# A two-layer diffusion trunk on one core: an earlier weight chunk and a one-run modulation in the first stage, and one ScalarE square moved behind branch A

## The chip, the core and the metric

The kernel runs on one core of a Trainium2 chip. The metric is device time in microseconds (us) of one execution, taken as a median of runs. Engines are named as the profile names them: PE is TensorE (matrix products), PEld its weight loads, ACT is ScalarE, DVE is VectorE, POOL is GpSimd, SP is the engine that issues nearly all DMAs.

## What is computed

Two layers over a latent stream `x` (256 tokens) and a context stream `ctx` (256 tokens), 2048 wide, all in fp32. Cut to what matters here:

```
shift, scale, gate = split(silu(c) @ w_mod[l] + b_mod[l])      # the same for the context with c_ctx
h    = rmsnorm(x, g_pre[l]) * (1 + scale) + shift              # h_c from ctx in the same way
proj = h @ w_in[l]                                             # a_u, a_v, a_g, q, k, v, b_g, c_x, c_g
y_a  = gelu(a_u) * (w_s @ rmsnorm(gelu(a_v)) + b_s) * silu(a_g)    # branch A
y_b  = window_attention(q, k, v, k_ctx, v_ctx) * silu(b_g)         # branch B
y_c  = (real part of fft2(c_x)) @ w_f * silu(c_g)                  # branch C
x    = x + gate * rmsnorm([y_a, y_b, y_c] @ w_out[l], g_post[l])   # ctx too, in the first layer only
```

## The kernel before, in words

Everything is laid out with the 2048 channels as 16 tiles of 128 (`k` = 0 to 15) and the tokens along the free axis (256 latent, 256 context). A product in fp32 is done as three passes in the PE's faster fp32r type: each operand is split into a rounded high part and a low remainder, and `mm3` (lines 428 to 430) adds high*high, low*high and high*low. Weights therefore take three steps: SP loads a 512 KB chunk into a `raw` buffer (line 383), ACT casts it to the high part `whi` (line 403), DVE subtracts to get the low part `wlo` (line 408). `Stream` hands the chunks out in a fixed order with `W.next()`; `W.emitting(512)` does cast and subtraction in halves of 512 columns, one step per `next`.

**First stage (layer 0).** The order of work on PE, ACT, DVE and SP is exactly the order in which the code is written (a manual schedule), up to `k` = 14. For each `k` the stage does four `start_av` products groups (branch A's `a_v`, one PSUM bank for each 128 tokens) and `start_au` for three heads of `a_u` (`au[0]` to `au[2]`; the third head, index 2, has its own weight chunk `ws_[2]`). Beside this, the modulation for the next tile `k + 1` is worked out: `mod_start` loads 2 MB of `w_mod` in pieces (line 162; tiles `mraw`, `macc`, `vv` for one parity of `k`, `mg`, `mgl`, `hh`, `hl` for the other), multiplies them on PE (line 169, `ps_mod`), transposes on DVE (line 173), gathers on PE (line 178, `ps_modc`), and adds biases on DVE (lines 187 to 190: `gs` and `sh`). `make_h` then makes the tile `h`: a DVE product (line 507), an ACT pass that rounds it (`hh`, line 511), a DVE pass for the remainder (`hl`, line 516). The generator is advanced by `take_in(n)`, n steps at a time; `h_next()` finishes it and makes `h`. `LOADS[k]` says how many weight chunks SP loads in step `k`, `SPLITS[k]` how many are cast and subtracted. `warm` (line 474) issues dummy bf16 products that write a bank which is overwritten later.

Before the change, the third head's first chunk is loaded and split in step `k` = 2; its products for `k` = 0, 1 and 2 stand together at the end of that step, and step 1 ends in four dummy products. The modulation that step 2 works out (for `k` = 3) is multiplied in two runs of two pieces, one after each half of the `a_v` products.

**The border of layer 1.** In the last steps of layer 1's own first stage the context stream's residual is finished in the background (`boundary_ctx`): DVE multiplies (line 1176), POOL issues DMAs that add the old stream into `yo` (line 1168), ACT squares the result (line 1185), and DVE sums the squares. Here the queue order comes from a scheduler, with `boundary_ctx` at lowered priority. Branch A begins with Gelu on ACT (lines 755 and 757), squares with a sum along the row (line 759), a power on POOL (line 459) and a scaling on DVE (line 763); PE then mixes positions (`ps_mix`, line 768). `ps_mix` and branch C's `ps_mg` (line 783; read by ACT line 445 and DVE line 446) share two PSUM banks.

Of the kernel before, what the change touches and what calls it, by code (L numbers as in the profile page):

```python
# [10 lines left out]
AF = mybir.ActivationFunctionType  # L11
# [55 lines left out]
def trunk_kernel(ctx: ExitStack, tc: tile.TileContext, xT, xhalf, cT, wss, wsl, wmod, win, wout0, wout1, const, vec, rows,  # L67
                 wmat, bs, sink, out):
    nc = tc.nc
    V, A, G, PE, DMA = nc.vector, nc.scalar, nc.gpsimd, nc.tensor, nc.sync  # L70
# [22 lines left out]
    yo = [sb([P, T], F32, f"yo{k}") for k in range(KT)]  # L93
# [180 lines left out]
    state = {"ctx": [], "phase": "", "owed": 0.0}  # L274
# [6 lines left out]
                k1=2.5, v1=2.5, q1=1, bg1=0.3, out1=1.4)  # L281
    NEAR = [0] * 14 + [1, 2, 3]

    LOADS = [1, 1, 1, 2, 1, 1, 1, 1, 1, 0, 2, 0, 1, 1, 1, 0]
    SPLITS = [1, 1, 1, 2, 0, 1, 1, 1, 1, 1, 0, 2, 0, 1, 1, 1]
    MIDDLE, EARLY = 3, 4
    LOWC = 60
    YT = 3.0
# [54 lines left out]
    class Stream:  # L343
# [75 lines left out]
        def next(self):  # L419
            self.fetch()  # L420
            pace()
            self.pos += 1
            return self.out[self.pos - 1]

    W = Stream()
# [45 lines left out]
    def warm(ps, n):  # L471

        for _ in range(n):
            PE.matmul(ps, wz[:, 0:P], wz, start=True, stop=True)
# [102 lines left out]
    def layer(l):  # L577
# [13 lines left out]
        av = [mm_ps("av") for _ in range(nt)]  # L591
# [17 lines left out]
        def start_au(k, heads=(0, 1, 2)):  # L609
            for j in heads[:3 - l]:  # L610
                if j == 2:
                    c, auw = slice((k % 8) * P, (k % 8 + 1) * P), ws_[2]
                else:
                    c, auw = slice((k % 4) * 256 + j * P, (k % 4) * 256 + (j + 1) * P), ws_[1]
                if last:
                    mm2(au[j], part(auw, c), hh[k], k)
                else:
                    mm3(au[j], part(auw, c), (hh[k], hl[k]), k == 0, k == KT - 1)
            later.tick(PASS * 512 * nt + PASS * n * 2)

        if l == 0:
            made = {}

            def mod_in(k, n=5):
                if k < KT:
                    g = made.setdefault(k, mod_start(k, 1))
                    for _ in range(n):
                        next(g, None)

            for k in range(KT):  # L630
                def take_in(n):
                    mod_in(k + 1, n)

                def splits():
                    for _ in range(SPLITS[k]):
                        W.emit()

                def h_next():

                    if k + 1 < KT:  # L640
                        mod_in(k + 1)
                        make_h(0, k + 1, rb0, [0, 1])

                if k % 2 == 0:
                    take(k)
                if k <= EARLY:
                    take_in(1)
                if k >= EARLY:
                    mod_in(k + 2, 1)
                for _ in range(LOADS[k]):  # L650
                    W.load()
                if k == 0:
                    start_av(0, range(nt))
                    take_in(3)
                    e = W.emitting(512)
                    next(e)
                    next(e)
                    take_in(2)
                    take(0, (1,))
                    start_au(0, (0,))  # L660
                    h_next()
                    list(e)
                    start_au(0, (1,))
                    warm(au[2], 3)
                elif k < MIDDLE:
                    start_av(k, range(nt // 2))
                    take_in(2)
                    start_av(k, range(nt // 2, nt))
                    take_in(1)
                    splits()  # L670
                    take_in(2)
                    start_au(k, (0,))
                    h_next()
                    start_au(k, (1,))
                    if k == 1:
                        warm(au[2], 4)
                    else:
                        ws_[2] = W.next()
                        for i in range(k + 1):
                            start_au(i, (2,))  # L680
                else:
                    start_av(k, range(nt // 2))
                    if k <= EARLY:
                        take_in(3)
                        splits()
                        take_in(2)
                        start_av(k, range(nt // 2, nt))
                        h_next()
                    else:
                        if k == KT - 2:  # L690
                            first_stage.close()
                        if k + 2 < KT:
                            banks["mod", k + 2] = banks["modc", k + 1] = ms_ps("mod")
                        splits()
                        mod_in(k + 2, 4)
                        if k + 1 < KT:
                            mod_in(k + 1)
                            make_h(0, k + 1, rb0, [0, 1])
                        mod_in(k + 2, 1)
                        start_av(k, range(nt // 2, nt))  # L700
                    if k >= KT - 2:
                        for _ in range(2):
                            with low(LAG), tc.issue_after(W.last.ins):
                                next(mods)
                    take(k, (1, 2))
                    start_au(k)
                    if k == EARLY:
                        mod_in(k + 2, 5)
# [42 lines left out]
        def branch_a():  # L751
            vt = [w2k([P, 512]) for _ in range(nt)]
            ss = sb([P, 4], F32, "ss")
            for j in range(len(au)):
                A.activation(ytmp(j), joined(au[j]) if last else au[j], AF.Gelu_apprx_tanh)
            for t in range(nt):
                A.activation(vt[t], av[t], AF.Gelu_apprx_tanh)
            for t in range(nt):
                A.activation(av[t], vt[t], AF.Square, accum_out=ss[:, t:t + 1])
            r = rstd_cols(ss[:, 0:nt], nt, 512)  # L760
            state["norm"] = state["pow"]
            for t in range(nt):
                V.tensor_scalar(out=vt[t], in0=vt[t], scalar1=r[:, t:t + 1], scalar2=None, op0=ALU.mult)
            yield 11.0 if l == 0 else 7.0
            for h in range(4):
                ps = ms_ps("mix")
                for t in range(nt):
                    PE.matmul(ps[:, t * P:(t + 1) * P], vt[t][:, h * P:(h + 1) * P], ws[:, h], start=True, stop=True)
                m = w2k([P, nt, P])
                V.scalar_tensor_tensor(out=m, in0=ps[:, 0:n].rearrange("p (t q) -> p t q", q=P),  # L770
                                       scalar=vc(l, "gsgu")[:, h:h + 1],
                                       in1=bsb[:, h].unsqueeze(1).to_broadcast([P, nt, P]),
                                       op0=ALU.mult, op1=ALU.add)
                V.tensor_tensor(out=ytmp(h), in0=ytmp(h), in1=m.rearrange("p t q -> p (t q)"), op=ALU.mult)
                yield (4.0 if h == 1 else 2.0) if l == 0 else (7.0 if h == 1 else 2.0)
# [389 lines left out]
    def boundary_ctx(acc):  # L1165

        def add(k):
            G.dma_start(yo[k][:, CTX], xhalf[1, k // 4][:, k % 4], accum_op=ALU.add)

        r = sb([P, S], F32, "rbs", 2)  # L1170
        r0 = yield from rms_of(1, acc[:, CTX], 3.2)
        A.copy(r, r0)
        acc1 = acc[:, CTX]
        for k in range(KT + LATE):
            if k < KT:
                V.tensor_tensor(out=yo[k][:, CTX], in0=yo[k][:, CTX], in1=r, op=ALU.mult)
                if k < 8:
                    add(k)
                else:
                    with tc.issue_after(state["norm"].ins):  # L1180
                        add(k)
            i = k - LATE
            if i >= 0:
                q = w2k([P, S]) if i else acc1
                A.activation(q, yo[i][:, CTX], AF.Square)
                if i:
                    V.tensor_tensor(out=acc1, in0=acc1, in1=q, op=ALU.add)
            if k % 2:
                yield YX1 if k == 7 else YC
        yield YE  # L1190
        r0 = yield from rms_of(1, acc1, 6.0)
        r = sb([P, S], F32, "rbs", 2)
        V.tensor_copy(r, r0)
        for i, k in enumerate([12, 13, 14, 15] + list(range(12))):
            make_h(1, k, r, [1])
            state["ctx"].append(k)
            if i % 2:
                yield YH
# [145 lines left out]
```

## Time and profile before

| what | us |
|---|---|
| median of 3 runs | 1138.46 (1137.81 to 1140.13) |
| the profiled execution, as timed | 1138.35 |
| its span in the trace, first to last instruction | 1136.6 |
| PE, PEld busy | 1123.4, 931.8 |
| DVE, ACT, POOL busy | 879.8, 514.4, 32.5 |

The profiled execution lies 0.11 us from the median. Times in the text are from the start of the span. A row of the timeline gives start, duration, engine, line, operation, the tile written and read, and the shapes; in brackets stands the idle time of that engine before it and what ended it. A PE product of 512 columns is shown with a duration of about 0.39 us, but products overlap: in a run of them one starts every 0.23 us. So starts are compared here, not durations.

### The profile page before, as it was taken

How to read it: one execution, taken by the hardware profiler on the slowest of the kernel's cores; microseconds unless marked ns; L12 is line 12 of the kernel's file. 1: busy time of each engine (PE TensorE's matmuls, PEld its weight loads, DVE VectorE, ACT ScalarE, POOL GpSimd, SP SyncE). 2: the span in 40 equal slices, each digit the busy share in tenths (PEclk: the TensorE clock that was granted, in tenths of full speed). 3: DMA queues.
4: the chain of work that ended last, by engine and by line, in shares of the span. 5: the costliest groups of instructions: out<-in, count | busy, mean ns of one | idle time of the engine just before them, and what ended most of it. 6: DMA issues, size and time to landing. Idle time of an engine off the chain costs nothing.

```text
span 1136.6 us, 16851 instructions
## 1 busy us (share of the span) xinstructions
PE 1123.4 (99%) x6335; PEld 931.8 (82%) x6339; DVE 879.8 (77%) x1480; ACT 514.4 (45%) x933; POOL 32.5 (3%) x39
## 2 busy tenths in 40 slices
PE   8999999999999999999999999999999999999997
PEld 3567788888898888888888888987898988888885
DVE  1545499999987887888998994396788689868884
ACT  5322422332325667632532323365655369856550
POOL 0000000000000000000000000205000000000001
PEclk9999999999999999999999999999999999999999
DMA  9999766556655343355566655268756675555972
GB/s 354 393 379 404 252 204 195 178 186 212 212 168 184 112 139 114 118 188 186 164 205 203 218 191 166 72 197 203 221 179 206 224 268 193 174 160 195 299 256 74
DMA packets 72658, 234.28 MB, mean 206 GB/s; under 512 B 8448, under 2 KB 11392, under 8 KB 72576
## 3 DMA queue, kind: packets, MB, share of 16 engines
q1 hardware_dynamic: 70272, 231.11, 61.3%
q0 software_dynamic: 2304, 2.10, 1.2%
q8 instruction: 49, 0.80, 0.3%
q14 instruction: 33, 0.27, 0.1%
HBM read 231.08 MB, written 2.10 MB: 205 GB/s over the span
## 4 chain that ended last, share of the span: by engine, by line
PE 96%; DMA 2%; DVE 0%; SPq 0%; issue 0%; ACT 0%; POOL 0%; DVEq 0%; POOLq 0%
PE ps_t L428 14%; PE ps_t L429 14%; PE ps_t L430 14%; PE ps_t L545 10%; PE ps_t L546 5%; PE ps_y L428 3%; PE ps_y L430 3%; PE ps_y L429 3%; PE ps_mod L169 2%; PE ps_av L428 2%; PE ps_cx L430 2%; PE ps_cx L428 2%; PE ps_cx L429 2%; PE ps_av L429 2%; PE ps_av L430 2%; PE ps_tp L917 2%
## 5 line engine op out<-in xcount | busy, mean ns | idle before, releaser
L403 ACT CAST whi<-raw 128x1024 fp32r<-128x1024 f32 (+1 forms) x216 | 224.2, 1041 | 323.1 <-PE ps_t L429 188.7
L408 DVE TENSOR_TENSOR wlo<-raw,whi 128x1024 fp32r<-128x1024 f32 (+1 forms) x216 | 260.6, 1210 | 64.5 <-ACT whi L403 63.0
L428 PE MATMUL ps_t<-hh,whi 128*128 128x512 f32 (+1 forms) x704 | 268.1, 381 | 0.0
L430 PE MATMUL ps_t<-hh,wlo 128*128 128x512 f32 (+1 forms) x704 | 267.6, 380 | 0.0
L429 PE MATMUL ps_t<-hl,whi 128*128 128x512 f32 (+1 forms) x704 | 267.4, 380 | 0.0
L207 DVE SCALAR_TENSOR_TENSOR macc<-mraw,cs,macc 128x512 f32<-128x512 f32 x360 | 249.2, 746 | 17.8 <-DMA mraw<-in_wmod_dram 17.4
L545 PE MATMUL ps_t<-hh,whi 128*128 128x512 f32 x448 | 163.8, 403 | 0.0
L430 PEld LDWEIGHTS ps_t<-hh,wlo 128*128 128x128 f32 x704 | 132.4, 188 | 25.3
L428 PEld LDWEIGHTS ps_t<-hh,whi 128*128 128x128 f32 x704 | 132.4, 188 | 24.7 <-issue 0.8
L429 PEld LDWEIGHTS ps_t<-hl,whi 128*128 128x128 f32 x704 | 132.4, 188 | 23.5
L546 PE MATMUL ps_t<-hh,wlo 128*128 128x256 f32 x448 | 125.7, 281 | 0.0
L545 PEld LDWEIGHTS ps_t<-hh,whi 128*128 128x128 f32 x448 | 84.2, 188 | 19.2 <-issue 0.5
L546 PEld LDWEIGHTS ps_t<-hh,wlo 128*128 128x128 f32 x448 | 84.7, 189 | 0.5 <-issue 0.5
L511 ACT ACTIVATE hh<-w2k,sh 128x256 fp32r<-128x256 f32 x48 | 21.8, 502 | 79.2 <-DVE w2k L507 79.2
L428 PE MATMUL ps_y<-whi,hh 128*128 128x512 f32 x104 | 41.3, 397 | 0.0
L430 PE MATMUL ps_y<-whi,hh 128*128 128x512 f32 x104 | 40.6, 390 | 0.0
L428 PE MATMUL ps_av<-whi,hh 128*128 128x512 f32 x96 | 39.9, 416 | 0.6 <-ACT hh L511 0.6
L429 PE MATMUL ps_y<-wlo,hh 128*128 128x512 f32 x104 | 40.5, 389 | 0.0
L428 PE MATMUL ps_cx<-whi,hh 128*128 128x512 f32 x96 | 38.7, 403 | 0.0
L429 PE MATMUL ps_av<-wlo,hh 128*128 128x512 f32 x96 | 37.9, 394 | 0.0
L429 PE MATMUL ps_cx<-wlo,hh 128*128 128x512 f32 x96 | 37.3, 389 | 0.0
L445 ACT CAST w2k<-ps_tp 128x512 fp32r<-128x512 f32 x40 | 23.4, 584 | 23.1 <-PE ps_scc L429 12.7
(398 smaller groups left out, 1859.0 us busy)
## 6 DMA issues: line engine op xcount, KB each, us to landing
raw<-in_win_dram SPq DMA_DIRECT2D x160, 512.0 KB, 4.3
mraw<-in_wmod_dram SPq DMA_DIRECT2D x128, 512.0 KB, 4.5
raw<-in_wout_dram SPq DMA_DIRECT2D x60, 512.0 KB, 4.3
mraw<-in_wsl_dram SPq DMA_DIRECT2D x16, 512.0 KB, 7.7
yo<-in_xT_dram SPq DMA_DIRECT2D x16, 256.0 KB, 5.3
macc<-in_wsl_dram SPq DMA_DIRECT2D x8, 512.0 KB, 7.8
vv<-in_wsl_dram SPq DMA_DIRECT2D x8, 512.0 KB, 8.2
mg<-in_wsl_dram SPq DMA_DIRECT2D x8, 512.0 KB, 8.3
```

The source lines that it names most:

```text
L169: PE.matmul(ps[32 * kk:32 * kk + 32, 0:n], cpad[:, kg * 4 + kk], ws[kk], start=kg == 0, stop=kg == 3, tile_position=(0, 32 * kk))
L207: V.scalar_tensor_tensor(out=acc[:, s], in0=w[:, kk % 2], scalar=c, in1=acc[:, s], op0=ALU.mult, op1=ALU.add)
L403: A.copy(ph, rc)
L408: self.last = V.tensor_tensor(out=pl, in0=rc, in1=ph.bitcast(F32), op=ALU.subtract)
L428: PE.matmul(ps, st[0], mv[0], start=start, stop=False)
L429: PE.matmul(ps, st[0], mv[1], start=False, stop=False)
L430: PE.matmul(ps, st[1], mv[0], start=False, stop=stop)
L445: A.copy(hi, src)
L511: first = A.activation(h_of(l, k, sl)[0], t[:, sl], AF.Identity, bias=sh[l][:, k, s:s + 1])
L545: PE.matmul(ps, w[0], h, start=k == 0, stop=False)
L546: PE.matmul(ps[:, 0:S], w[1], h[:, 0:S], start=False, stop=k == KT - 1)
L917: PE.transpose(tp[:, (2 * j + b) * P:(2 * j + b + 1) * P], src, ident)
```

## The change

Four edits in the first stage and one at the border.

- The third head's first weight chunk is loaded in step 1 instead of step 2, right behind that step's own chunk. Its first half is cast and subtracted at the end of step 1, its second half in step 2 (`list(e)`).
- The third head's products for `k` = 0 and `k` = 1 take the place of the four dummy products at the end of step 1; step 2 keeps only its own.
- In step 2 all four pieces of the modulation for `k` = 3 are multiplied in one run behind the first half of the `a_v` products (`take_in(4)`).
- Step 2's `a_v` chunk is taken with `W.next()` in step 1 (`ahead`), so that the stream's order stays the same.
- At the border, the context's squares may not be queued on ACT ahead of branch A's last square (`state["gelu"]`).

```
-    LOADS = [1, 1, 1, 2, 1, 1, 1, 1, 1, 0, 2, 0, 1, 1, 1, 0]
-    SPLITS = [1, 1, 1, 2, 0, 1, 1, 1, 1, 1, 0, 2, 0, 1, 1, 1]
+    LOADS = [1, 2, 0, 2, 1, 1, 1, 1, 1, 0, 2, 0, 1, 1, 1, 0]
+    SPLITS = [1, 1, 0, 2, 0, 1, 1, 1, 1, 1, 0, 2, 0, 1, 1, 1]
...
-                if k % 2 == 0:
+                if k == 2:
+                    ws_[0] = ahead
+                elif k % 2 == 0:
                     take(k)
...
                 elif k < MIDDLE:
                     start_av(k, range(nt // 2))
-                    take_in(2)
+                    if k == 2:
+                        list(e)
+                    take_in(2 if k == 1 else 4)
                     start_av(k, range(nt // 2, nt))
                     take_in(1)
-                    splits()
-                    take_in(2)
+                    if k == 1:
+                        splits()
+                        take_in(2)
+                        e = W.emitting(512)
+                        next(e)
+                        next(e)
                     start_au(k, (0,))
                     h_next()
                     start_au(k, (1,))
                     if k == 1:
-                        warm(au[2], 4)
-                    else:
+                        ahead = W.next()
                         ws_[2] = W.next()
-                        for i in range(k + 1):
-                            start_au(i, (2,))
+                        start_au(0, (2,))
+                    start_au(k, (2,))
...
             for t in range(nt):
-                A.activation(av[t], vt[t], AF.Square, accum_out=ss[:, t:t + 1])
+                state["gelu"] = A.activation(av[t], vt[t], AF.Square, accum_out=ss[:, t:t + 1])
...
-                A.activation(q, yo[i][:, CTX], AF.Square)
+                with tc.issue_after(state["gelu"].ins):
+                    A.activation(q, yo[i][:, CTX], AF.Square)
```

What stands on DVE around step 1's end, before (`raw_371` is step 1's own chunk, `raw_447` the third head's, `ps_modc` the modulation for `k` = 2, and the rows of lines 507 and 516 make `h` of `k` = 2):

```order
L408 TENSOR_TENSOR wlo_399<-raw_371,whi_398 128x1024
L173 STREAM_TRANSPOSE w2k_406<-ps_mod_379 128x256
L187 SCALAR_TENSOR_TENSOR gs_26_90<-ps_modc_411,vecs_78 128x2
L189 TENSOR_TENSOR gs_26_90<-gs_26_90,vecs_78 128x2
L190 TENSOR_TENSOR sh_28_92<-ps_modc_411,vecs_78 128x2
L507 SCALAR_TENSOR_TENSOR w2k_421<-yo_3_63,gs_26_90,acc_241 128x256 x2
L516 SCALAR_TENSOR_TENSOR hl_103_420<-w2k_421,sh_28_92,hh_102_419 128x256 x2
L408 TENSOR_TENSOR hh_115_476<-raw_447,hh_113_474 128x512
L408 TENSOR_TENSOR hl_116_477<-raw_447,hl_114_475 128x512
```

And with the change (the third head's chunk is now `raw_373`):

```order
L408 TENSOR_TENSOR wlo_401<-raw_371,whi_400 128x1024
L173 STREAM_TRANSPOSE w2k_408<-ps_mod_381 128x256
L408 TENSOR_TENSOR hh_104_412<-raw_373,hh_102_410 128x512
L187 SCALAR_TENSOR_TENSOR gs_26_90<-ps_modc_419,vecs_78 128x2
L189 TENSOR_TENSOR gs_26_90<-gs_26_90,vecs_78 128x2
L190 TENSOR_TENSOR sh_28_92<-ps_modc_419,vecs_78 128x2
L507 SCALAR_TENSOR_TENSOR w2k_429<-yo_3_63,gs_26_90,acc_241 128x256 x2
L516 SCALAR_TENSOR_TENSOR hl_108_428<-w2k_429,sh_28_92,hh_107_427 128x256 x2
L408 TENSOR_TENSOR hl_105_413<-raw_373,hl_103_411 128x512
```

The first half's subtraction moved ahead of the whole chain that makes `h` of `k` = 2; the second half's stays behind it. On ACT the cast of the first half moves in the same way, ahead of the two passes of line 511.

What SP issues at that place, before:

```order
L383 DMA raw_371<-in_win_dram 128x1024
L162 DMA mg_435<-in_wsl_dram 128x1024
L162 DMA mgl_437<-in_wsl_dram 128x1024
L162 DMA hh_107_439<-in_wsl_dram 128x512
L162 DMA hl_108_441<-in_wsl_dram 128x512
L162 DMA hh_109_443<-in_wsl_dram 128x512
L162 DMA hl_110_445<-in_wsl_dram 128x512
L383 DMA raw_447<-in_win_dram 128x1024
L162 DMA mraw_520<-in_wsl_dram 128x1024
```

And with the change:

```order
L383 DMA raw_371<-in_win_dram 128x1024
L383 DMA raw_373<-in_win_dram 128x1024
L162 DMA mg_445<-in_wsl_dram 128x1024
L162 DMA mgl_447<-in_wsl_dram 128x1024
L162 DMA hh_112_449<-in_wsl_dram 128x512
L162 DMA hl_113_451<-in_wsl_dram 128x512
L162 DMA hh_114_453<-in_wsl_dram 128x512
L162 DMA hl_115_455<-in_wsl_dram 128x512
L162 DMA mraw_516<-in_wsl_dram 128x1024
```

The third head's chunk passed the six pieces of the modulation for `k` = 3 (2 MB); everything behind them keeps its place.

What stands on ACT at the border, before (`acc` is the context's first square, the two rows that read `ps_av` are the Gelus of `a_v`, and those that write it are branch A's squares):

```order
L403 CAST whi_7045<-raw_7043 128x1024
L1185 ACTIVATE acc_5257<-yo_945_5338 128x256
L757 ACT_TABLE_LOAD
L757 ACTIVATE w2k_7137<-ps_av_6742 128x512
L403 CAST whi_7091<-raw_7089 128x1024
L551 COPY join_7140<-ps_au_6744 128x256
L551 COPY join_7144<-ps_au_6745 128x256
L757 ACTIVATE w2k_7138<-ps_av_6743 128x512
L759 ACTIVATE ps_av_6742,ss_7139<-w2k_7137 128x512
L759 ACTIVATE ps_av_6743,ss_7139<-w2k_7138 128x512
```

And with the change (the square is the last row; all later squares keep their places):

```order
L403 CAST whi_7041<-raw_7039 128x1024
L764 ACT_TABLE_LOAD
L764 ACTIVATE w2k_7133<-ps_av_6738 128x512
...
L403 CAST whi_7179<-raw_7177 128x1024
L445 CAST mg_7131<-ps_mg_7187 128x4x128
L445 CAST mg_7131<-ps_mg_7193 128x4x128
L403 CAST whi_7214<-raw_7212 128x1024
L551 COPY join_7207<-ps_t_7154 128x256
L1193 ACTIVATE acc_5253<-yo_945_5334 128x256
```

One square of the sixteen moved, from ahead of the Gelu table's load to sixteen rows later, behind the join of the next head.

## The prediction

> **What bounds the kernel now.** I read the chain of work that ended last first, then the clock, then every wait of PE.
>
> ```profile
> PEclk9999999999999999999999999999999999999999
> PE 96%; DMA 2%; DVE 0%; SPq 0%; issue 0%; ACT 0%; POOL 0%; DVEq 0%; POOLq 0%
> ```
>
> PE is the chain for 96% of the span, at a granted clock of 0.9 or more in every slice. So time can only come from products that go, or from moments in which PE stands still. The waits list few of those. In 60 to 120 us PE waited for data twice:
>
> ```profile
> PEld ps_mod L169 <- DMA vv<-in_wsl_dram: 0.3, 1, 0.3
> PEld ps_mod L169 <- DMA hl<-in_wsl_dram: 0.2, 1, 0.2
> ```
>
> These are 0.5 us for pieces of the modulation, so there the DMAs and PE arrive almost together. The windows around them (columns: window, length, busy PE, PEld, DVE, ACT, POOL with instruction counts, PE clock, DMA share, GB/s):
>
> ```profile
> 53.00:66.00 13.00, 13.00 (x120) 8.57 (x116) 5.14 (x16) 2.76 (x5) 0.00 (x0) 1.00 0.97 324
> 66.00:122.00 56.00, 56.00 (x503) 40.55 (x492) 28.87 (x74) 13.96 (x24) 0.00 (x0) 1.00 1.03 404
> ```
>
> From 66 us the DMAs run at 404 GB/s; in the 13 us before they ran at 324, because SP waited for buffers that PE had not yet released. That gap is worth 13 x (1 - 324/404) = 2.6 us of transfers. It decides the first part below.
>
> The one large stall of PE is at the border of layer 1:
>
> ```profile
> 787.09 0.28 PE L546 MATMUL ps_t<-hh,wlo 128*128 128x256 f32 x1
> 788.66 0.71 PE L768 MATMUL ps_mix<-ws,w2k 128*128 128x128 f32 x4 [1.30 <-DVE mgl L446]
> ```
>
> 1.30 us idle, 1.57 us from start to start.
>
> **First stage, part by part.** PE's rows from the end of step 1 to the modulation in step 3:
>
> ```profile
> 39.95 0.40 PE L430 MATMUL ps_au<-hh,wlo 128*128 128x512 f32 x1
> 40.41 0.81 PE L474 MATMUL ps_au<-join 128*128 128x512 bf16 x3
> 40.99 0.50 PE L428 MATMUL ps_av<-whi,hh 128*128 128x512 f32 x1
> ...
> 42.65 0.64 PE L169 MATMUL ps_mod<-mg,kt 128*32 128x256 f32 x8
> ...
> 43.65 0.50 PE L428 MATMUL ps_av<-whi,hh 128*128 128x512 f32 x1
> ...
> 45.24 0.41 PE L169 MATMUL ps_mod<-hh,kt 128*32 128x256 f32 x2
> ...
> 46.24 0.50 PE L428 MATMUL ps_au<-hh,whi 128*128 128x512 f32 x1
> ...
> 47.13 0.24 PE L178 MATMUL ps_modc<-w2k,cst 128*32 128x4 f32 x8
> ...
> 48.11 0.40 PE L428 MATMUL ps_au<-hh,hh 128*128 128x512 f32 x1
> ...
> 50.16 0.39 PE L428 MATMUL ps_av<-whi,hh 128*128 128x512 f32 x1
> ...
> 51.61 1.07 PE L169 MATMUL ps_mod<-mraw,kt 128*32 128x256 f32 x16
> ...
> 53.47 0.50 PE L428 MATMUL ps_av<-whi,hh 128*128 128x512 f32 x1
> ```
>
> The third head's nine products take 50.16 - 48.11 = 2.05 us, 0.23 each. Six of them (1.37 us) move to where the dummies were, starting at 39.95 + 0.23 = 40.18 and ending at 41.55. Step 2's `a_v` began at 40.99, so it is 0.56 later. The dummies themselves give nothing back beyond the 0.81 us between 40.18 and 40.99: behind them PE waited for `h` of `k` = 2 anyway, as ACT's rows show (the first and third are casts of weight chunks, the others the rounding passes of `h`).
>
> ```profile
> 35.86 1.05 ACT L403 CAST whi<-raw 128x1024 fp32r<-128x1024 f32 x1 [1.93 <-DMA raw<-in_win_dram]
> 40.43 0.91 ACT L511 ACTIVATE hh<-w2k,sh 128x256 fp32r<-128x256 f32 x2 [3.53 <-DVE w2k L507]
> 42.59 0.62 ACT L403 CAST hh<-raw 128x512 fp32r<-128x512 f32 x1 [1.25 <-DMA raw<-in_win_dram]
> ...
> 48.36 0.91 ACT L511 ACTIVATE hh<-w2k,sh 128x256 fp32r<-128x256 f32 x2 [4.62 <-DVE w2k L507]
> ```
>
> `a_v` of step 2 started 0.56 us after ACT began that `h` (40.43 to 40.99); I use this distance once more below.
>
> One run instead of two: the two take 43.65 - 42.65 and 46.24 - 45.24, 1.00 each; step 3's single run takes 53.47 - 51.61 = 1.86. A break in the flow of products costs more than itself: the first half of `a_v` takes 1.66 behind a wait (40.99 to 42.65) and 1.45 behind other products (50.16 to 51.61), 0.21 more. I take 0.2 for the switch of shapes that the single run saves, too, an estimate. So one run saves 2.00 - 1.86 + 0.2 = 0.34, and the third-head products that now lead straight into step 2 save 0.21. Together 0.55 against 0.56 lost: `ps_modc`, which gathers the modulation for `k` = 3, stays at 47.13.
>
> Behind it step 2 has three third-head products instead of nine, so PE is ready for step 3 at 48.11 + 0.68 = 48.79, 1.37 us early. What is late next is `h` of `k` = 3: it hangs on `ps_modc`, so ACT still begins it at 48.36 and `a_v` can start at 48.36 + 0.56 = 48.92. Behind a wait its half takes 1.66, so step 3's modulation starts at 50.58 instead of 51.61. **PE gains 1.03 us.**
>
> Do the moved weights come in time? The chunk before landed by 35.86 and the old third-head chunk by 42.59, with 2.5 MB between them, 1.35 us for each 512 KB. Directly behind, it lands near 37.2, an estimate. ACT is idle from 36.91 to 40.43, so the 0.62 us cast is covered. DVE:
>
> ```profile
> 39.52 0.16 DVE L187 SCALAR_TENSOR_TENSOR gs<-ps_modc,vecs 128x2 f32<-128x2 f32 x1 [0.63 <-PE ps_modc L178]
> ...
> 43.24 0.69 DVE L408 TENSOR_TENSOR hh<-raw,hh 128x512 fp32r<-128x512 f32 x1 [1.38 <-ACT hh L403]
> ```
>
> The subtraction (0.69) now stands ahead of `gs`, where DVE idled 0.63; I cost it at nothing, at most 0.06. Three new waits lie here, all for that one landing: ACT's cast, with the passes of `h` for `k` = 2 queued behind it; DVE's subtraction, with `gs` and the rest of the same chain behind it; and PE's first third-head product, with step 2's `a_v` behind it. By the times above the chunk is cast by 37.9 and subtracted by 39.6, before PE asks at 40.18. The six modulation pieces that SP issues behind the chunk land 1.35 us later, the last by about 42.6 instead of 41.3; PE reads it after 43.0 + 0.9. SP passes the chunk over those six issues only; behind them its order is the same, and POOL's queue is not touched.
>
> Can the 1.03 us survive 66 us, where PE already waited for transfers? The pieces involved are issued when PE releases their buffers, so with PE 1.03 earlier they are issued 1.03 earlier, into a gap of 2.6 us. From below: they land when they did, and the gain is 0. From above: the gap closes further and the 0.5 us of waits goes too, 1.5. I take **1.2 us**, the pure shift and a third of the waits.
>
> **Border.** ACT's rows:
>
> ```profile
> 778.16 0.42 ACT L1185 ACTIVATE acc<-yo 128x256 f32<-128x256 f32 x1 [3.94 <-DMA yo<-in_xhalf_dram]
> 778.59 1.28 ACT L757 ACT_TABLE_LOAD   x1
> 779.89 0.60 ACT L757 ACTIVATE w2k<-ps_av 128x512 f32<-128x512 f32 x1
> ...
> 784.17 2.01 ACT L403 CAST whi<-raw 128x1024 fp32r<-128x1024 f32 x2
> 786.06 1.09 ACT L445 CAST mg<-ps_mg 128x512 fp32r<-128x512 f32 x2
> ```
>
> ACT stood 3.94 us before the square, waiting for POOL's addition to land, with branch A queued behind. Without the square the table loads from 774.22 to 775.5. The Gelu then waits for PE:
>
> ```profile
> 776.86 0.39 PE L430 MATMUL ps_av<-whi,hh 128*128 128x512 f32 x1
> ```
>
> The first bank's last product is three earlier, at 776.17, so Gelu can start near 776.65, 3.2 us earlier than 779.89. Everything queued behind it on ACT, the casts of 784.17 and 786.06 among them, can move by as much. What follows on DVE, and what POOL does meanwhile:
>
> ```profile
> 783.79 0.17 DVE L456 TENSOR_SCALAR rs_a<-ss 128x2 f32<-128x2 f32 x1 [0.45 <-ACT ps_av L759]
> 784.86 0.88 DVE L763 TENSOR_SCALAR w2k<-w2k,rs_b 128x512 f32<-128x512 f32 x2 [0.90 <-POOL rs_b L459]
> 785.66 2.35 DVE L408 TENSOR_TENSOR wlo<-raw,whi 128x1024 fp32r<-128x1024 f32 x2
> 787.93 1.28 DVE L446 TENSOR_TENSOR mgl<-ps_mg,mg 128x512 fp32r<-128x512 f32 x2
> ```
>
> ```profile
> 772.64 7.37 POOL L1168 DMA_DIRECT2D yo<-in_xhalf_dram  x8 [5.85 <-DVE yo L1176]
> ```
>
> Moved by 3.2, `rs_a` stands at 780.6, just after POOL's eight issues end at 780.01 (the power for `rs_b` is queued behind them); the scaling goes to 781.7, the two subtractions to 782.5, and `mgl`, whose first half frees the bank that `ps_mix` needs, to 784.8, done by 785.5. PE asks at 787.1: 1.6 us to spare, so the stall goes whole. The square itself, 0.42 us, now lies behind a join and before line 940's pass, where PE waits for nothing. **Gain 1.4 us**, between the row's 1.30 idle and 1.57 start to start; from below 0, if a new wait takes its place.
>
> **Sum.** 1138.35 - 1.2 - 1.4 = 1135.75; the median of the runs is 0.11 above that execution, so **1135.8**. Its own range is 1135.2 to 1136.5.
>
> **A rule against the change.** The Trainium skill's page "TensorE: Matmul & The Clock Gate", section "Part 1: The HAM clock gate", says that an idle window of about 3.4 us halves PE's clock; dummies guard against that. In the forecast PE idles only from 48.79 to 48.92, so the rule changes nothing there. In the third rival PE would stand from 40.18 to 43.9, 3.7 us, and the rule would add up to 1.7 us to it (half of 3.4, an estimate from the page), about 1141.8. The windows above show the clock at 1.00 throughout, and no idle time of that length behind 53 us, so no row here tests it.
>
> **Rivals.** *Transfers hold the first stage.* PE arrives at 66 us 1.03 early and waits there for the same landings: `hl` and `vv` cost 1.5 us instead of 0.5, and only the border pays, 1138.46 - 1.4 = 1137.1. For it speak the two waits above, against it the window at 324 GB/s, which leaves room for earlier issues.
>
> *The border's stall stays,* because the two weight casts ahead of `ps_mg` need chunks that come no earlier (ACT reads them at 784.17 without a wait, so the rows don't show how long they lay there): 1138.46 - 1.2 = 1137.3.
>
> *Slower: the moved weights come late.* DVE works its rows in order, so `gs` stands behind the subtraction. It decides from a landing after 39.52 - 0.69 - 0.62 = 38.2, 1.0 us later than I expect. Landing at 42.59 as before, `gs` starts at 43.9 instead of 39.52, `a_v` of step 2 4.4 later; 0.34 and 1.03 come back: +3.0, less the border's 1.4: 1140.1.
>
> **How the numbers follow.** Forecast 0.64, transfers 0.16, stall stays 0.12, slower 0.05, both gains gone 0.03. The range reaches to the first two rivals and to both upper bounds (1138.46 - 1.5 - 1.57 = 1135.4, less run spread): 1134.9 to 1137.5. A measurement tells about 0.2% from no change, 2.3 us, so 1136.2 is the limit; some of the forecast's own range lies above it. Faster 0.56, same 0.39, slower 0.05.
>
> **What would show it.** Line 446's wait before `ps_mix` gone and Gelu near 776.65 less the first gain (1.2); step 3's modulation 1.0 us earlier; the third head's cast near 37.2; window 53 to 66 above 324 GB/s. Wrong if PE's waits on `hl` and `vv` grow by about 1 us, if `gs` of step 1 waits for line 408, or if `ps_mix` waits for another name.

## The result, and the profile after

| | before | changed |
|---|---|---|
| median of 22 runs each, us | 1138.70 (1136.53 to 1140.13) | 1136.39 (1135.30 to 1137.70) |
| ratio, 95% interval | | 0.9982 (0.9976 to 0.9988) |
| profiled execution, us | 1138.35 | 1136.23 |
| its span in the trace, us | 1136.6 | 1134.5 |

The change saves 2.3 us, 0.18%. The interval does not contain 1, so the gain is real, though its size lies just inside the 0.2% that the prediction took as the limit of what can be told; with 22 runs each the limit was finer than that (the interval is 0.06% wide to each side). 1136.39 is 0.6 above the forecast and inside its range.

The page of the changed kernel: its span, the clock and the chain by engine.

```profile
span 1134.5 us, 16841 instructions
PEclk9999999999999999999999999999999999999998
PE 97%; DMA 2%; DVE 0%; SPq 0%; ACT 0%; issue 0%; POOL 0%; DVEq 0%; POOLq 0%
```

PE still bounds the kernel. Two executions of one kernel differ by more than the change is worth, as the last experiment shows, so I read the first stage from one landmark to another: from step 1's `ps_modc` to step 3's modulation. In the kernel before the first landmark is this row of PE:

```profile
31.29 0.24 PE L178 MATMUL ps_modc<-w2k,cst 128*32 128x4 f32 x8
```

From here to step 3's modulation (51.61, shown in the prediction) it took 20.32 us. PE's rows in the changed kernel:

```profile
31.88 0.24 PE L178 MATMUL ps_modc<-w2k,cst 128*32 128x4 f32 x8
...
39.78 0.24 PE L178 MATMUL ps_modc<-w2k,cst 128*32 128x4 f32 x8
...
40.77 0.39 PE L428 MATMUL ps_au<-hh,hh 128*128 128x512 f32 x1
...
41.91 0.39 PE L430 MATMUL ps_au<-hh,hh 128*128 128x512 f32 x1
42.14 0.39 PE L428 MATMUL ps_av<-whi,hh 128*128 128x512 f32 x1
...
43.59 0.64 PE L169 MATMUL ps_mod<-mg,kt 128*32 128x256 f32 x8
...
45.46 0.50 PE L428 MATMUL ps_av<-whi,hh 128*128 128x512 f32 x1
...
47.72 0.24 PE L178 MATMUL ps_modc<-w2k,cst 128*32 128x4 f32 x8
...
49.51 0.51 PE L428 MATMUL ps_av<-whi,hh 128*128 128x512 f32 x1
...
51.17 1.07 PE L169 MATMUL ps_mod<-mraw,kt 128*32 128x256 f32 x16
```

51.17 - 31.88 = 19.29 us: 1.03 less, the size that the prediction gave. The first landmark itself stands 0.59 later: PE idles 0.86 us at 30.73 for a cast whose weight chunk SP issued at 20.67, ahead of the moved chunk (28.14), and the border's part alone, with the old order of loads, idles 0.85 us there too. `ps_modc` for `k` = 3 stands 15.84 behind the first landmark in both kernels (47.13 - 31.29, 47.72 - 31.88). The third head's weights, on ACT and on DVE:

```profile
37.73 0.62 ACT L403 CAST hh<-raw 128x512 fp32r<-128x512 f32 x1 [0.23 <-DMA raw<-in_win_dram]
41.00 0.91 ACT L511 ACTIVATE hh<-w2k,sh 128x256 fp32r<-128x256 f32 x2 [2.66 <-DVE w2k L507]
...
48.94 0.91 ACT L511 ACTIVATE hh<-w2k,sh 128x256 fp32r<-128x256 f32 x2 [6.52 <-DVE w2k L507]
```

```profile
39.40 0.65 DVE L408 TENSOR_TENSOR hh<-raw,hh 128x512 fp32r<-128x512 f32 x1
40.09 0.16 DVE L187 SCALAR_TENSOR_TENSOR gs<-ps_modc,vecs 128x2 f32<-128x2 f32 x1
```

They landed at 37.7 (37.1 without the 0.59; 37.2 was forecast), and `gs` stands 8.21 behind the first landmark (40.09 - 31.88), before 8.23 (39.52 - 31.29): not delayed. The last row of ACT is `h` of `k` = 3: step 3's `a_v` starts 0.57 behind it (48.94 to 49.51), so PE is held by it. Behind the first stage, the windows (the columns are those of the prediction):

```profile
53.00:66.00 13.00, 13.00 (x120) 8.65 (x116) 5.31 (x17) 2.75 (x5) 0.00 (x0) 1.00 1.00 359
66.00:122.00 56.00, 56.00 (x498) 41.02 (x491) 29.63 (x74) 13.96 (x24) 0.00 (x0) 1.00 1.03 403
```

The gap that SP left is smaller, 359 GB/s in place of 324, and PE's waits for `vv` and `hl` are no longer in the list. At the border, ACT, then DVE, then PE:

```profile
773.75 1.28 ACT L764 ACT_TABLE_LOAD   x1
776.12 0.60 ACT L764 ACTIVATE w2k<-ps_av 128x512 f32<-128x512 f32 x1 [1.09 <-PE ps_av L430]
...
786.43 0.42 ACT L1193 ACTIVATE acc<-yo 128x256 f32<-128x256 f32 x1
```

```profile
780.23 0.17 DVE L456 TENSOR_SCALAR rs_a<-ss 128x2 f32<-128x2 f32 x1 [0.42 <-ACT ps_av L766]
...
784.36 1.28 DVE L446 TENSOR_TENSOR mgl<-ps_mg,mg 128x512 fp32r<-128x512 f32 x2
```

```profile
786.73 0.60 PE L775 MATMUL ps_mix<-ws,w2k 128*128 128x128 f32 x4
```

The table is loaded during the old wait, the Gelu waits for PE alone, the square comes 10 us behind the Gelu, and `ps_mix` has no bracket: the stall is gone. PE runs 0.49 ahead of the kernel before as it comes here (its row for `ps_rb` at 739.44 in place of 739.93), so the Gelu was due at 776.65 - 0.49 = 776.16 and `rs_a` at 780.1.

### The profile page after: what moved, and what is told of

Its sections match the earlier page's. It is cut to its first block, busy times and chain, and to the rows that moved or that the text cites. A ratio compares the mean times of both kernels' runs of the same rounds, so it can differ in the third digit from the quotient of the medians.

```text
span 1134.5 us, 16841 instructions
## 1 busy us (share of the span) xinstructions
PE 1122.2 (99%) x6332; PEld 932.0 (82%) x6335; DVE 879.7 (78%) x1480; ACT 514.6 (45%) x933; POOL 33.0 (3%) x39
## 4 chain that ended last, share of the span: by engine, by line
PE 97%; DMA 2%; DVE 0%; SPq 0%; ACT 0%; issue 0%; POOL 0%; DVEq 0%; POOLq 0%
PE ps_t L428 14%; PE ps_t L429 14%; PE ps_t L430 14%; PE ps_t L545 10%; PE ps_t L546 5%; PE ps_y L428 3%; PE ps_y L430 3%; PE ps_y L429 3%; PE ps_mod L169 2%; PE ps_av L428 2%; PE ps_cx L428 2%; PE ps_cx L430 2%; PE ps_cx L429 2%; PE ps_av L429 2%; PE ps_av L430 2%; PE ps_tp L924 2%
```

## Experiments

All runs are read by three stretches of PE between landmarks, and by their medians. A: step 1's `ps_modc` to step 3's modulation. B: from there to the first `ps_cx` (near 150 us). C: the boundary's `ps_rb` (near 740 us) to `ps_mix`. Beside them stands the landing of POOL's first addition to `yo`, from its issue. All in us; A, B and C are differences of two starts in the run's trace. "Tied" is a kernel in which no square of the context stands ahead of the Gelu and waits.

| trace | A | B | C | landing |
|---|---|---|---|---|
| before | 20.32 | 98.57 | 48.73 | 5.50 |
| before again | 20.32 | 98.35 | 48.66 | 5.39 |
| before, third | 20.31 | 98.23 | 48.57 | 5.33 |
| without dummies | 20.32 | 98.46 | 48.88 | 5.59 |
| one run | 19.94 | 98.23 | 48.08 | 4.79 |
| border only (tied) | 20.31 | 98.44 | 47.33 | 5.56 |
| border, other data (tied) | 20.31 | 98.22 | 47.34 | 5.38 |
| changed (tied) | 19.29 | 98.24 | 47.29 | 4.86 |
| changed again (tied) | 19.27 | 98.23 | 47.33 | 5.55 |
| first stage only | 19.28 | 98.26 | 47.34 | 3.71 |
| two runs (tied) | 19.64 | 98.24 | 47.32 | 5.36 |
| chunk behind 2 pieces (tied) | 20.34 | 98.24 | 47.34 | 4.91 |
| chunk behind 6 pieces (tied) | 23.71 | 98.25 | 47.30 | 4.45 |
| the same, with dummies (tied) | 23.07 | 98.25 | 47.33 | 5.46 |

### First stage alone

```
-                with tc.issue_after(state["gelu"].ins):
-                    A.activation(q, yo[i][:, CTX], AF.Square)
+                A.activation(q, yo[i][:, CTX], AF.Square)
```

> The changed kernel with the square back in its old place: the first stage's edits alone. If the two parts add up, as the prediction has it: counted from the end of the start-up (about 32 us), step 3's modulation comes 1.0 us earlier, PE is 1.35 us ahead by 130 us, gives 0.27 back at ps_z near 242 us, where PE now waits for DVE, and meets the border's stall unchanged: 1.1 us faster than the kernel before, ratio 0.9990. Theory of chance at the start: the 0.59 us that PE lost at 30.7 us in the changed kernel's trace is not there, or not in all of these runs. Rivals: the loads' new order causes that loss, then ps_au starts at 30.7 here too and the gain is 0.5; or transfers hold the first stage and nothing is gained.

1137.66 us against 1138.49 of the kernel before on the same chip, ratio 0.9989 (0.9980 to 0.9998): 0.8 us where 1.1 was expected, inside the interval. A is 19.28, so the part works by itself. The loss at 30.7 us is not there: it comes and goes (0 to 0.9 us in the traces, with the old order of loads and with the new), so the new order does not cause it. PE gives 0.3 back at `ps_z` near 242 us, as expected, but so does the kernel before in its second trace (0.3 against its first), so this need not come from PE's being early. One thing I had not expected: C is 47.34, without a stall, though the square stands in its old place. ACT's row, POOL's, and PE's:

```profile
776.82 0.42 ACT L1192 ACTIVATE acc<-yo 128x256 f32<-128x256 f32 x1 [2.16 <-DMA yo<-in_xhalf_dram]
```

```profile
773.08 4.67 POOL L1175 DMA_DIRECT2D yo<-in_xhalf_dram  x5 [5.85 <-DVE yo L1183]
```

```profile
787.65 0.60 PE L775 MATMUL ps_mix<-ws,w2k 128*128 128x128 f32 x4
```

(POOL's row merges the issues in the stretch that was asked for; there are eight in all, as in the prediction's row.) The addition landed 3.7 us behind its issue, not 5.5 as in the trace that the prediction used. The stall is no constant.

### Border alone

```
+                state["gelu"] = A.activation(av[t], vt[t], AF.Square, accum_out=ss[:, t:t + 1])
...
+                with tc.issue_after(state["gelu"].ins):
+                    A.activation(q, yo[i][:, CTX], AF.Square)
```

> The kernel before with the square tied behind branch A's last square, and nothing else. Theory: the stall of ps_mix goes whole, 1.45 us, ratio 0.9987; everything up to 770 us as before, ps_z near 242 us without a wait, since PE is not early there. Rival: an earlier first stage is needed for the casts of the weights to come in time, then part of the stall is left (0.5 us or more) and the gain is under 1.0.

1137.76 against 1138.49, ratio 0.9994 (0.9986 to 1.0003): too small to be told by the time. In the trace the landing took 5.56, among the latest, and C is 47.33: no stall. The border's part needs nothing from the first stage.

### Is it the wait or the place?

```
-                A.activation(q, yo[i][:, CTX], AF.Square)
+                A.activation(q, yo[i][:, CTX if i else LAT], AF.Square)
```

> The kernel before, but the first of the context's squares reads the latent half of the same tile, which is long there, in place of the half that POOL's addition writes: it leaves out one tile's context squares from the sum. The square stays ahead of branch A on ACT (some casts earlier), the wait for the landing is gone. Theory: the wait is what costs, not the place: Gelu starts near 776.6 and the stall of ps_mix goes whole, 1.45 us. Rival: the work queued ahead of the Gelu counts; then the Gelu stays near 779 and the gain is under 0.4.

This kernel leaves one tile's context squares out of the sum. 1137.73 against 1138.53, ratio 0.9995 (0.9986 to 1.0004). ACT's rows:

```profile
765.74 0.40 ACT L1185 ACTIVATE acc<-yo 128x256 f32<-128x256 f32 x1
...
777.27 0.60 ACT L757 ACTIVATE w2k<-ps_av 128x512 f32<-128x512 f32 x1 [1.09 <-PE ps_av L430]
```

The square is ahead of the Gelu and the Gelu waits for PE alone; C is 47.34. (PE was 0.6 later here at `ps_rb` than in the kernel before, hence 777.27 in place of 776.6.) The scheduler put the square three casts earlier, so the place is not exactly the old one, and its 0.40 us fall into time in which ACT idles; but a square ahead of the Gelu that waits for no landing leaves no stall, so the wait for the landing is what cost.

### How large is the stall?

No edit: the kernel before, twice more.

> The kernel before, unchanged, for its trace: how large is the border's stall in another execution? Four traces without the tie show, from the addition's issue on POOL to its landing, 5.50, 3.71, 4.79 and 5.59 us, and stalls of ps_mix of 1.47, 0, 0.75 and 1.56 us. If the stall is this landing less 4.03 us, and nothing below that, it is so here too, and step 3's modulation starts 20.32 us after step 1's ps_modc, as in the first trace. Rival: the stall is 1.47 whatever the landing.

> The same once more: stall of ps_mix = landing of the addition less 4.03 us (0 if that is negative); 20.32 us from step 1's ps_modc to step 3's modulation. Rival: 1.47 whatever the landing.

One execution each: 1138.29 and 1138.63 us.

ACT's row, POOL's and PE's of the first of the two:

```profile
778.20 0.42 ACT L1185 ACTIVATE acc<-yo 128x256 f32<-128x256 f32 x1 [3.83 <-DMA yo<-in_xhalf_dram]
```

```profile
772.78 5.59 POOL L1168 DMA_DIRECT2D yo<-in_xhalf_dram  x6 [5.85 <-DVE yo L1176]
```

```profile
788.71 0.71 PE L768 MATMUL ps_mix<-ws,w2k 128*128 128x128 f32 x4 [1.19 <-DVE mgl L446]
```

`ps_mix` starts 1.36 later than without a wait (1.19 idle and 0.17 of a broken flow), and 5.39 - 4.03 = 1.36. In the third trace: 1.29 against 5.33 - 4.03 = 1.30. So in all six traces without the tie the stall is the landing less 4.03 us, or nothing: 1.47, 1.36, 1.29, 1.56, 0.75 and 0, to 0.02 us. By the table these six have a C of 48.38 in the mean; the tied ones have 47.32, whatever the landing. **The border is worth 1.06 us in the mean of these six, between 0 and 1.56.** Only three of the six are the kernel before itself; these have a C of 48.65, which makes the border worth 1.33. The small stalls (0.75 and 0) come from edited kernels. That one program's landing moves is shown by the changed kernel (4.86 and 5.55), but what moves it, chance, the chip or the program, is open. A is 20.32 and 20.31, as expected.

### Two runs again, one run alone

In the changed kernel, two runs:

```
-                    take_in(2 if k == 1 else 4)
+                    take_in(2)
                     start_av(k, range(nt // 2, nt))
                     take_in(1)
+                    if k == 2:
+                        take_in(2)
```

> The changed kernel with step 2's modulation for k = 3 in two runs of 8 products again, as before; all other edits stay. The prediction's term: the switch into and out of the second run costs 0.34 us (0.14 by the rows, 0.20 estimated). Theory: ps_modc and the h of k = 3 that hangs on it come 0.34 later, and PE, which waits for that h, with them: 0.34 slower than the changed kernel (0.03%, read in the trace from the rows 39.8 to 51.2, as the time can't tell it). Rivals: only the 0.14 of the rows; or nothing, as DVE's transpose waits for both halves anyway.

In the kernel before, one run:

```
-                    take_in(2)
+                    take_in(2 if k == 1 else 4)
                     start_av(k, range(nt // 2, nt))
                     take_in(1)
                     splits()
-                    take_in(2)
+                    if k == 1:
+                        take_in(2)
```

> The kernel before with step 2's modulation in one run of 16 products, and nothing else: no weights ahead, third-head products where they were. Theory: PE is the chain in step 2, so step 3's modulation comes 0.34 us earlier than in the kernel before, and the rest of the first part's 1.0 is not there. Rivals: 0.14; or the whole gain of the first stage comes from this run (1.0) and the moved products add nothing.

1136.92 (ratio 0.9986, 0.9977 to 0.9995) and 1138.11 (1.0000, 0.9991 to 1.0008), both against 1138.53. PE's rows with two runs, then with one run in the kernel before:

```profile
31.47 0.24 PE L178 MATMUL ps_modc<-w2k,cst 128*32 128x4 f32 x8
...
47.68 0.25 PE L178 MATMUL ps_modc<-w2k,cst 128*32 128x4 f32 x8
...
51.11 1.07 PE L169 MATMUL ps_mod<-mraw,kt 128*32 128x256 f32 x16
```

```profile
32.16 0.24 PE L178 MATMUL ps_modc<-w2k,cst 128*32 128x4 f32 x8
...
47.62 0.24 PE L178 MATMUL ps_modc<-w2k,cst 128*32 128x4 f32 x8
```

From one `ps_modc` to the other it is 16.21 and 15.46, against 15.84 in both kernels: the second run costs 0.37 in the one and 0.38 in the other, and the estimate was 0.34. A follows: 19.64 and 19.94. So the moved products without the single run gain 0.68 (20.32 - 19.64), and the single run is the rest.

### The dummies

```
-                        warm(au[2], 4)
+                        pass
```

> The kernel before without the four dummy products of step 1, and nothing else. The prediction said that they give nothing back, since PE waits for h of k = 2 behind them. Theory: a_v of step 2 starts when it did (0.56 after ACT begins that h), time the same within 0.1 us. Rival: PE comes 0.8 us earlier. Rival by the clock-gate rule of the Trainium skill's page on the clock gate: PE stands still for 0.8 us only, far below the window it names, so the clock stays.

1139.35 against 1138.53, ratio 1.0005 (0.9997 to 1.0014); A is 20.32, to the hundredth what it is with them. ACT's row and PE's:

```profile
40.72 0.91 ACT L511 ACTIVATE hh<-w2k,sh 128x256 fp32r<-128x256 f32 x2 [3.51 <-DVE w2k L507]
```

```profile
41.28 0.50 PE L428 MATMUL ps_av<-whi,hh 128*128 128x512 f32 x1 [0.64 <-ACT hh L511]
```

`a_v` starts 0.56 behind ACT's `h`, with dummies or without. Their place was free.

### The chunk behind two pieces

The third head's chunk goes into SP's row behind two of the six modulation pieces for `k` = 3:

```
-    LOADS = [1, 2, 0, 2, ...
+    LOADS = [1, 1, 0, 2, ...
...
+                issued.append(k0)
+                if issued.count(3) == 2 and k0 == 3:
+                    W.load()
...
-                if k <= EARLY:
+                if k <= EARLY and k != 2:
                     take_in(1)
...
+                if k == 1:
+                    mod_in(3, 1)
```

The last lines let step 1 issue the six pieces, so that they can stand ahead of the chunk; the rest of SP's order is that of the changed kernel.

> The changed kernel, but SP issues the third-head chunk behind two of the six modulation pieces (512 KB each, 1.28 us each by the landings of the changed kernel). The chunk lands 2.56 us later, near 40.2, where the prediction put the limit at 38.2. Theory of DVE's order: gs stands behind the subtraction (landing + 0.62 + 0.69), so it starts 1.5 us later than in the changed kernel, and step 2 and all behind it 1.5 later: 1.5 to 1.9 slower than the changed kernel, 0.4 to 0.8 faster than the one before. Rival: only PE's third-head products wait, 0.9. Rival: the chunk is not needed that early, 0.

1137.48 against 1138.49, ratio 0.9993 (0.9984 to 1.0001). A is 20.34, 1.05 more than in the changed kernel: less than the 1.5 of my theory, more than PE's own wait. ACT's rows, DVE's, and PE's:

```profile
39.65 0.62 ACT L408 CAST hh<-raw 128x512 fp32r<-128x512 f32 x1 [2.78 <-DMA raw<-in_win_dram]
41.82 0.91 ACT L516 ACTIVATE hh<-w2k,sh 128x256 fp32r<-128x256 f32 x2 [1.54 <-DVE w2k L512]
```

```profile
40.31 0.69 DVE L413 TENSOR_TENSOR hh<-raw,hh 128x512 fp32r<-128x512 f32 x1 [1.45 <-ACT hh L408]
40.92 0.15 DVE L192 SCALAR_TENSOR_TENSOR gs<-ps_modc,vecs 128x2 f32<-128x2 f32 x1
```

```profile
42.38 0.50 PE L433 MATMUL ps_av<-whi,hh 128*128 128x512 f32 x1
```

(The first landmark is at 31.25 in this trace.) `gs` stands 9.67 behind it, 1.46 later than in the changed kernel, as the theory says. But there `a_v` starts 1.14 behind ACT's `h` (41.00 to 42.14), since PE is busy with the six moved products; here it is 0.56 (41.82 to 42.38). So 0.58 of the delay falls into slack that I had left out, and the break in the flow takes 0.21 back: 1.46 - 0.58 + 0.21 = 1.09, measured 1.05.

### The chunk behind all six pieces, and the clock

The same with `issued.count(3) == 6`.

> The changed kernel, but SP issues the third-head chunk behind all six modulation pieces (2 MB, 5.25 us by the landings of the changed kernel): landing near 42.9. This is the prediction's slower rival. Theory: gs starts near 44.2, 4.2 us later than in the changed kernel; PE stands still some 3.5 us ahead of the third head; the run is 4.2 us slower than the changed kernel, near 1140.5, 2 us slower than before. Rival by the clock-gate rule that the prediction cites from the Trainium skill ("TensorE: Matmul & The Clock Gate", "Part 1: The HAM clock gate"): the granted clock falls behind the idle time and products between 44 and 48 us take up to twice as long, up to 1.7 us more, near 1142.2.

1141.83 against 1138.49, ratio 1.0027 (1.0016 to 1.0039): slower than before. A is 23.71, 4.42 more than in the changed kernel. PE's rows, and ACT's for `h` of `k` = 2:

```profile
43.24 0.80 PE L433 MATMUL ps_au<-hh,hh 128*128 128x512 f32 x1 [2.74 <-ACT hh L408]
...
45.12 0.63 PE L434 MATMUL ps_au<-hl,hh 128*128 128x512 f32 x1
45.54 0.63 PE L435 MATMUL ps_au<-hh,hh 128*128 128x512 f32 x1
45.97 0.52 PE L433 MATMUL ps_av<-whi,hh 128*128 128x512 f32 x1
```

```profile
44.74 0.91 ACT L516 ACTIVATE hh<-w2k,sh 128x256 fp32r<-128x256 f32 x2 [1.54 <-DVE w2k L512]
```

Behind 2.74 us of idle time the products come every 0.43 us, not every 0.23, and the windows tell why (the column behind POOL's is the granted clock):

```profile
40.00:43.00 3.00, 0.51 (x3) 0.07 (x1) 0.00 (x0) 0.42 (x1) 0.00 (x0) 0.97 1.04 410
43.00:46.00 3.00, 2.75 (x7) 2.15 (x8) 2.56 (x8) 1.46 (x4) 0.00 (x0) 0.50 1.03 410
```

The clock is 0.50 from 43 to 46 us. To see whether the idle time is the cause, the next kernel fills it:

```
                         ws_[2] = W.next()
+                        warm(au[2], 12)
                         start_au(0, (2,))
```

> The kernel of the run before with the chunk behind all six pieces, and twelve dummy products (0.23 us each, 2.8 us) on PE in the idle time ahead of the third head's products. There the granted clock was 0.50 from 43 to 46 us, behind 2.74 us of idle PE, and the products came every 0.43 us. If the idle time is what lowers the clock, as the clock-gate rule has it: the clock is 1.00 in that window, the products come every 0.23 us, a_v of step 2 starts 0.56 us after ACT begins its h, 0.67 us earlier than without the dummies, and step 3's modulation 23.0 us after the start of step 1's ps_modc in place of 23.7. Rival: the slow products have another cause (the transfers that run beside them), then 23.7 stays.

```profile
40.00:43.00 3.00, 2.86 (x15) 1.10 (x13) 0.02 (x1) 0.62 (x1) 0.00 (x0) 1.00 1.02 406
43.00:46.00 3.00, 2.86 (x10) 1.65 (x11) 2.76 (x9) 1.42 (x3) 0.00 (x0) 1.00 1.04 414
```

The clock is 1.00 with the transfers at about the same rate, and A is 23.07: the slow clock cost 0.64 us. By the time the two can't be told apart (1140.89 against 1138.37 of before, ratio 1.0023, 1.0014 to 1.0032). The Trainium skill's page "TensorE: Matmul & The Clock Gate", section "Part 1: The HAM clock gate", gives an idle window of about 3.4 us. The trace agrees that idle time halves the clock (0.50), but 2.74 us was enough here (3.13 from start to start). The estimate from that page in the prediction was up to 1.7 us; the runs show 0.64. Step 2's `a_v` starts 1.23 behind ACT's `h` (44.74 to 45.97) and not 0.56, which is nearly all of it, and the clock was back by 46.3 us (from there on the products come every 0.23).

### The changed kernel once more

No edit.

> The changed kernel, unchanged, for a second trace. Theory: step 3's modulation starts 19.29 us after step 1's ps_modc, no stall at ps_mix whatever the landing of POOL's addition, and from ps_modc to the modulation nothing depends on how PE fared at 30 us. Open, since no theory of the change rests on it: POOL's power ahead of ps_rb near 739 us took 0.71 us in the kernel before (three traces) and in the changed one, 1.55 to 1.75 in eight other programs. If the program decides, it is 0.71 again; if chance does, it may be 1.6.

Its span is 1138.3 us, 3.8 more than that of the first trace of the same kernel. A, B and C are 19.27, 98.23 and 47.33: none of the 3.8 lies in what the change touches, and there is no stall though the landing took 5.55. Nearly all of it lies in the start-up (1.5 until step 1's `ps_modc`), in a product of `ps_z` near 233 us (1.2), which waits for DVE's subtraction, and ahead of `ps_rb` near 740 us (0.9). The last is POOL's power, here 1.65 us, which had been 0.71 in the first trace of the same kernel.

## Why the prediction was right, and where it was off

*One run for two, and moved products.* Right to 0.04 us: `ps_modc` for `k` = 3 stays, the single run saves 0.37 to 0.38, PE is held by `h` until 49.51 (48.92 + 0.59), and the gain is 1.03 in two traces of the changed kernel and in the first stage alone. That the dummies' place was free is shown.

*The weights in time.* Right for the landing, the cast, the subtraction and `gs`. The limit that I gave for the third rival, 38.2, is right for `gs` and 0.6 too early for PE: the step "`a_v` of step 2 4.4 later" for a `gs` 4.4 later left out that PE, busy with the six moved products, asks 0.58 later itself. The rival's mechanism is real, and its kernel slower than before: priced at 3.0 in the first stage, it measured 3.39 with the slow clock (23.71 - 20.32) and 2.75 without (23.07 - 20.32).

*Past 66 us.* "The pure shift and a third of the waits" was right in size, 1.2 against 1.17, by luck, as its reason was not right. The 1.03 survives whole up to 150 us, where B ends. The waits go whole too, but they are no fixed 0.5: B, over its floor of 98.23, has 0.34 in the trace that I read, and 0.12, 0, 0.23, 0.21 and 0 in the five other traces with the old order and two runs. Their mean is 0.15; with the new order it is 0.01. That the rival *transfers hold the first stage* is out follows from B. From there to `ps_rb` near 740 us no single trace can tell 1 us: that stretch took 589.75, 590.03 and 590.53 us in the three traces of the kernel before, 590.03 and 592.28 in the two of the changed one, mainly by waits of `ps_z` between 210 and 243 us and by POOL's power.

*Border.* The mechanism was right in each step: the wait gone, the Gelu, `rs_a` and `mgl` where they were put, the stall gone whole. **What was too certain is its size, "gain 1.4 us".** I took it from one execution, in which POOL's addition landed 5.50 us behind its issue. The stall is the excess of that landing over 4.03, and it moves: its mean is 1.06 over six traces, 1.33 over the three of the kernel before alone.

*The sum.* 1.03 + 0.14 + 1.06 = 2.23, or 2.50 with 1.33, against 2.31 measured (1.4 to 2.7 by the interval) and 2.6 forecast; the times can't tell these apart. Of the 0.6 us by which the forecast was low, 0.24 lies in its base: three runs of the kernel before had the median 1138.46, twenty-two have 1138.70.

*The chances.* With 0.56 on over 0.2% I stood 0.2 us from the limit; the case that came is "same" by that bound.

## What to carry to other kernels

A stall that ends with a transfer has a distribution and not a size: price its removal by several traces, or say how far its landing can move, before a row with two decimals goes into a sum. Work in an order written by hand repeats to 0.02 us between landmarks where no transfer is waited for (A), to 0.34 where one is (B), while the whole execution moves by 3.8 us; so read an edit of 0.1% from the landmarks on both sides of it. Before filling idle time or emptying it, ask which instruction behind it waits for another engine anyway: four dummies that cover such a wait are free, and so was the first 0.81 us of the six real products, which took 1.37.

## What the runs showed of the hardware

POOL's power (line 459) ahead of `ps_rb` took 0.71 us in five of fourteen traces and 1.55 to 1.75 in nine. The changed kernel's first trace, and the run with two runs:

```profile
738.63 0.71 POOL L459 TENSOR_TENSOR rs_b<-rs_a,mhalf 128x2 f32<-128x2 f32 x1 [3.31 <-DVE rs_a L456]
```

```profile
738.50 1.75 POOL L459 TENSOR_TENSOR rs_b<-rs_a,mhalf 128x2 f32<-128x2 f32 x1 [3.31 <-DVE rs_a L456]
```

Where it is long, PE waits, as in the second of the two:

```profile
740.30 0.71 PE L480 MATMUL ps_rb<-identr,rs_b 128*128 128x128 f32 x4 [0.84 <-POOL rs_b L459]
```

The same program had it both ways, so the program does not decide it; what does stays open. It moves PE's rows behind it by 0.8 to 1.0 us, nearly half of what the change is worth.
